# Two query projections of a windowed attention as one pair of seven half products

## The chip, the cores and the metric

The kernel runs on one core of one Trainium2 chip. The metric is device time in microseconds (us), the median of several executions. TensorE does the matmuls, VectorE and ScalarE the element-wise work and the reading of matmul results out of PSUM, and SyncE (SP) issues every transfer, in one queue. GpSimd does next to nothing here.

## The reference

One encoder block on x of 1024 tokens by 1024 features, float32:

```
h = RMSNorm(x)
[g_q, g_k, g_v, g_r, lr_f, lr_b, s_q, s_k, s_v, gate_a, gate_b] = split(h @ w_in)
A = gated linear attention, 4 heads, chunks, both directions     (g_q, g_k, g_v, g_r, lr_f, lr_b)
B = softmax attention, 8 query and 2 key/value heads of 128, blocks of 128 tokens,
    each block sees itself and its two neighbours; RMS-normed and rotated s_q, s_k; a sink logit
x = x + (sigmoid(gate_a) * (A @ w_o_gla) + sigmoid(gate_b) * (B @ w_o_swa)) @ w_out
x = x + (silu(h2 @ w_ff_gate) * (h2 @ w_ff_up)) @ w_ff_out,   h2 = RMSNorm(x)
```

The change concerns `s_q = h @ w`, with w of 1024 x 1024: the queries of the eight softmax heads. The kernel calls its two column halves `sq0` (heads 0 to 3) and `sq1` (heads 4 to 7).

## The kernel before

**Precision.** A float32 operand is split into two float32r parts, high and low: `h` is ScalarE's rounded copy, `l` VectorE's difference (`wunit`, L63 to L70, and `wsplit` for weights; `xsplit` for activations). A product is three matmuls: high x high, high x low, low x high. A weight unit is 128 x 512, 256 KB. The normalised activations are held as `xh`, `xl`: eight feature groups of 128 by two token halves of 512, without the token's inverse norm, which is applied when a result is read out (`rstdt` for token-major, `rstd` for feature-major results).

**Dense work as filler.** A list `dense` holds Python generators, each of which emits one matmul at a time: `proj_t` (token-major projections: v0, v1, skv, sq0, sq1, each once for each token half), `proj_f` (feature-major ones) and `first_halves` (the first product of twelve later pairs, L229). `fill(n)` emits the next n matmuls of that list. TensorE's order is exactly the order in which the code emits (`manual_schedule`). The other engines and the transfers are ordered by a planner, from its own idea of costs and by when operands are ready, except where `keep_in_program_order` or `issue_after` pins an instruction.

The gated attention and then the softmax attention run in numbered slots, as software pipelines. Each slot is cut into stages, and behind each stage a share of dense matmuls is emitted; `GF` and `SF` say how many a slot gets. In slot t of the softmax attention, group n (block n // 2, heads 4(n % 2) to 4(n % 2) + 3) passes: rotation of its queries in slot n + 1 (`a_rope`, VectorE), transposes in n + 2 (`a_turn`, L756, then a split of the result), scores in n + 3 (`a_scores`; VectorE's masked maximum, L774; then ScalarE's exponentials), transposes of the probabilities in n + 4 (`a_probs`, L813, split at L816 and L817), output in n + 5 (`a_out`). `prep(t)` (from L710) loads block t's queries from DRAM. `need(key)` emits twelve dense matmuls at a time until that result has been produced.

**Order of the dense list before:** v0 (both token halves), q1, k1, q2, k2, v1 (both), q3, k3, then for the first token half skv, sq0, sq1, then the same three for the second half, then the first halves. For the first token half `wkeep` splits a weight unit and stores both parts in DRAM (L162); for the second half `wagain` loads them (L170).

**Results through DRAM.** Every projection is read out of PSUM into a staging tile (four buffers), stored, and loaded by its user. x-tiles for loads share three buffers (`xn`).

**Sums of activations.** `x_sums` forms, during gated attention and one step a slot, differences of the normalised activations for the later pairs of seven half products (`xT1`, `x22`, `xT2`, `xT3`, `xT4`) and stores them in DRAM. In the last four slots of the softmax attention, T1 and 22 are loaded and split into the homes of `xh`, `xl` of the second token half (`xpart`, L843, L837).

**Pairs of seven half products.** Some of the later stages already multiply 2 x 2 blocks with seven products in place of eight (`seven`, `pair_T1` and so on).

Of the kernel before, what the change touches and what calls it, by code (L numbers as in the profile page):

```python
# [22 lines left out]
WARM = 10  # L23
GF = ((8, 34), (24, 21), (36, 18), (1 << 30, 11))
SF = ((2, 50), (9, 24), (18, 18), (1 << 30, 12))
PAD = 672
# [4 lines left out]
def body(tc, i, out):  # L31
    nc = tc.nc
    with ExitStack() as root:
# [12 lines left out]
        def mmtile(shape=(P, 512), dt=F32):  # L46
            return psm.tile(list(shape), dt, tag="mm", name=nm("mm"))
# [181 lines left out]
        def first_halves():  # L229
# [4 lines left out]
            def steps():  # L234
                for j in range(0, len(PAIRS), 2):
                    Y = [mmtile(), mmtile()]
                    for u in range(2):
                        for q in range(2):
# [16 lines left out]

        dense = []

# [323 lines left out]
        def g_turn(hd, c):  # L581
# [6 lines left out]
            for j in range(2):  # L588
                nc.sync.dma_start(out=scr["o", 2 * hd + j, c // 4][:, (c % 4) * P:(c % 4 + 1) * P], in_=os_[:, j])

        dense += [proj_t("v0", 0, 0), proj_t("v0", 0, 1), proj_f("q1", 2), proj_f("k1", 3), proj_f("q2", 4), proj_f("k2", 5),
                  proj_t("v1", 1, 0), proj_t("v1", 1, 1), proj_f("q3", 6), proj_f("k3", 7), *(proj_t(nme, n, s) for s in range(2)
                                                          for nme, n in (("skv", 2), ("sq0", 3), ("sq1", 4)))] + [first_halves()]

# [7 lines left out]
        def x_diff(key, k, d, a, b):  # L602
            tc.keep_in_program_order(nc.vector.tensor_tensor(d, a, b, op=ALU.subtract))
            put((key, k), d)

        def x_sums():
            for k in range(KT // 2):
                a = x_norm(k, 0)
# [38 lines left out]
        with tc.manual_schedule(engines={mybir.EngineType.PE}):  # L647
            fill(44)
            for t in range(last + 1):
                work = [[at[t, j]] for j in (0, 5, 4, 3, 2, 1) if (t, j) in at]  # L650
                if t in behind:
                    work = work or [[]]
                    work[-1].append(behind[t])
                slot([lambda v=v: [f(*a) for f, *a in v] for v in work], share(GF, t))
                if t:
                    next(sums, None)
# [147 lines left out]
        def a_probs(g, n, kb):  # L804
# [4 lines left out]
            if kb == a.b0:  # L809
                a.pts = []  # L810
            pt = (mmtile if kb == a.b0 and len(dense) == 1 else chtile)((P, 4, P))
            for h in range(4):
# [7 lines left out]
        def a_out(g, n):  # L820
# [7 lines left out]
            for h in range(4):  # L828
                nc.sync.dma_start(out=scr["b", 4 * g + h, n // 4][:, (n % 4) * P:(n % 4 + 1) * P],
                                  in_=ob[:, h])  # L830

        XT = {q: [] for q in ("T1", "T2", "22", "T3", "T4")}
        def xsplit(pool, th, tl, src):
            h = pool.tile([P, HT], FR, tag=th, name=nm(th))
            l = pool.tile([P, HT], FR, tag=tl, name=nm(tl))
            nc.scalar.activation(h, src, AF.Copy)
            nc.vector.tensor_tensor(l, src, h.bitcast(F32), op=ALU.subtract)  # L837
            return h, l

        homes = {"T1": (xp, "xh{}1", "xl{}1", 0), "22": (xp, "xh{}1", "xl{}1", 4),  # L840
                 "T3": (xp, "xh{}0", "xl{}0", 0), "T4": (xp, "xh{}0", "xl{}0", 4)}

        def xpart(q, k):  # L843
            r = xn.tile([P, HT], F32, tag="xn", name=nm("xn"))
            nc.sync.dma_start(out=r, in_=scr[f"x{q}", k])
            pool, th, tl, d = homes[q]
            XT[q].append(xsplit(pool, th.format(k + d), tl.format(k + d), r))

# [15 lines left out]
        with tc.manual_schedule(engines={mybir.EngineType.PE}):  # L864
            for t, v in enumerate(todo):
# [10 lines left out]
                slot([lambda u=u: [f(*a) for f, *a in u] for u in work], share(SF, t))  # L876
                if t >= 2 * KT + 2:
                    assert len(dense) == 1
                    for q in ("T1", "22"):
                        xpart(q, t - 2 * KT - 2)  # L880
        swas.close()
# [738 lines left out]
```

## Time and profile before

| what | value |
|---|---|
| median of 3 runs | 1607.52 us (1606.2 to 1608.94) |
| the profiled execution | 1607.29 us |
| its span, first to last instruction | 1605.5 us |
| TensorE busy | 1596.9 us (99%), 7532 matmuls |
| VectorE busy | 1209.1 us (75%) |
| ScalarE busy | 903.5 us (56%) |
| moved by transfers | 323.24 MB |

The profile is of one execution. Its own time is what the run took on the device; the span is what lies between its first and last instruction. "Busy" is the union of an engine's instructions; matmuls overlap in it, so a busy TensorE may still start them at different rates. Lines such as L756 are lines of the kernel's file. In a row of a group of instructions stand line, engine, operation, output and inputs, shape and count, then busy us and the mean ns of one, then the idle time of the engine just before them and what ended it. A row of stretches gives the length, the busy time of each engine with its number of instructions, the granted TensorE clock as a share of full speed, the share of the 16 transfer engines and GB/s.

### The profile page before, as it was taken

To read this page: it belongs to the slowest core of one execution; us is meant where nothing else is said; L and a number is where in the kernel's file an instruction comes from. 1 tells how busy PE (TensorE), PEld (TensorE's weight loads), DVE (VectorE), ACT (ScalarE), POOL (GpSimd) and SP (SyncE) were. 2 spreads that over 40 slices of the span, in tenths; PEclk is the share of its full clock that TensorE was granted. 3 is DMA by queue.
4 is the path that set the end of the run, shared out by engine and by line. 5 is a ranking of instruction groups with operands and counts; after the bars stand their busy time and mean duration, and the time that the engine had idled before them with its cause. 6 is when DMAs were issued, how large, how long until landed. Compare 5 with 4: busy or idle time off the path is not lost.

```text
span 1605.5 us, 23093 instructions
## 1 busy us (share of the span) xinstructions
PE 1596.9 (99%) x7532; PEld 1330.1 (83%) x7532; DVE 1209.1 (75%) x2287; ACT 903.5 (56%) x1859; POOL 0.2 (0%) x4
## 2 busy tenths in 40 slices
PE   9999999999999999999999999999999999999999
PEld 6888888888888788888888888888888888888887
DVE  8568888746999678786855877777777878689655
ACT  7456778755998645455633656844444444354442
POOL 0000000000000000000000000000000000000000
PEclk9999999999999999999999999999999999999999
DMA  8856767888544487868733656634344564695433
GB/s 270 301 196 213 248 216 259 285 264 286 173 145 139 152 291 246 273 228 273 243 124 105 220 186 204 202 114 151 112 145 157 191 202 161 207 330 175 151 99 118
DMA packets 197979, 323.24 MB, mean 201 GB/s; under 512 B 23423, under 2 KB 49919, under 8 KB 197858
## 3 DMA queue, kind: packets, MB, share of 16 engines
q1 hardware_dynamic: 197858, 321.77, 60.8%
q8 instruction: 59, 0.97, 0.2%
q14 instruction: 62, 0.51, 0.1%
HBM read 216.29 MB, written 105.39 MB: 200 GB/s over the span
## 4 chain that ended last, share of the span: by engine, by line
PE 95%; DVE 2%; ACT 1%; DMA 1%; issue 0%; SPq 0%; DVEq 0%; ACTq 0%
PE mm L73 22%; PE mm L916 10%; PE mm L915 10%; PE mm L914 10%; PE ch L73 8%; PE mm L1458 7%; PE ch L1458 6%; PE ch L914 5%; PE ch L916 5%; PE ch L915 5%; PE mm L246 4%; PE ch L813 1%; PE ch L585 0%; PE ch L756 0%; PE ch L490 0%
## 5 line engine op out<-in xcount | busy, mean ns | idle before, releaser
L893 ACT ACTIVATE wh<-ws 128x512 fp32r<-128x512 f32 x164 | 103.2, 630 | 157.4 <-PE mm L915 83.8
L73 PE MATMUL mm<-wh,xl 128*128 128x512 f32 x320 | 127.3, 398 | 0.0
L73 PE MATMUL mm<-wh,xh 128*128 128x512 f32 x320 | 126.9, 397 | 0.3 <-ACT lrt L313 0.3
L73 PE MATMUL mm<-wl,xh 128*128 128x512 f32 x320 | 127.1, 397 | 0.0
L894 DVE TENSOR_TENSOR wl<-ws,wh 128x512 fp32r<-128x512 f32 x164 | 112.2, 686 | 15.8 <-ACT wh L893 15.4
L67 ACT ACTIVATE wh<-wr 128x512 fp32r<-128x512 f32 x114 | 71.1, 630 | 55.2 <-issue 16.9
L69 DVE TENSOR_TENSOR wl<-wr,wh 128x512 fp32r<-128x512 f32 x114 | 77.9, 686 | 22.0 <-ACT wh L67 20.5
L893 ACT ACTIVATE wh<-a 128x512 fp32r<-128x512 f32 x66 | 41.6, 632 | 90.3 <-PE mm L1458 42.7
L893 ACT ACTIVATE wh<-wr 128x512 fp32r<-128x512 f32 x76 | 47.9, 631 | 60.9 <-PE mm L915 20.2
L894 DVE TENSOR_TENSOR wl<-a,wh 128x512 fp32r<-128x512 f32 x66 | 45.5, 690 | 40.4 <-ACT wh L893 40.2
L73 PEld LDWEIGHTS mm<-wh,xh 128*128 128x128 f32 x320 | 60.3, 188 | 10.6 <-ACT lrt L313 0.8
L1458 PE MATMUL mm<-hl,wh 128*128 128x512 f32 x176 | 68.6, 390 | 0.0
L1458 PE MATMUL mm<-hh,wl 128*128 128x512 f32 x176 | 68.6, 390 | 0.0
L1458 PE MATMUL mm<-hh,wh 128*128 128x512 f32 x176 | 68.5, 389 | 0.0
L73 PEld LDWEIGHTS mm<-wl,xh 128*128 128x128 f32 x320 | 60.3, 188 | 9.6
L73 PEld LDWEIGHTS mm<-wh,xl 128*128 128x128 f32 x320 | 60.3, 188 | 9.0
L907 DVE TENSOR_TENSOR ws<-wr,wr 128x512 f32<-128x512 f32 x80 | 54.5, 686 | 8.0 <-DMA wr<-in_w_f_dram 4.0
L894 DVE TENSOR_TENSOR wl<-wr,wh 128x512 fp32r<-128x512 f32 x76 | 51.9, 684 | 7.6 <-ACT wh L893 7.0
L1425 DVE TENSOR_TENSOR hl<-hr,hh 128x512 fp32r<-128x512 f32 x77 | 52.8, 686 | 5.1 <-ACT hh L1424 5.1
L1424 ACT ACTIVATE hh<-hr 128x512 fp32r<-128x512 f32 x77 | 47.6, 619 | 7.9 <-DMA hr<-B 4.1
L1458 PE MATMUL ch<-hh,wh 128*128 128x512 f32 x132 | 51.4, 389 | 0.0
L1458 PE MATMUL ch<-hh,wl 128*128 128x512 f32 x132 | 51.4, 389 | 0.0
(449 smaller groups left out, 4910.1 us busy)
## 6 DMA issues: line engine op xcount, KB each, us to landing
wr<-in_w_fi_dram SPq DMA_DIRECT2D x110, 256.0 KB, 4.0
wr<-in_w_f_dram SPq DMA_DIRECT2D x96, 256.0 KB, 3.7
wh<-wh SPq DMA_DIRECT2D x80, 256.0 KB, 3.3
wl<-wl SPq DMA_DIRECT2D x80, 256.0 KB, 3.1
B<-c SPq DMA_DIRECT2D x44, 256.0 KB, 2.1
T<-st SPq DMA_DIRECT2D x44, 256.0 KB, 3.1
a<-in_w_fo_dram SPq DMA_DIRECT2D x44, 256.0 KB, 5.1
hr<-T SPq DMA_DIRECT2D x44, 256.0 KB, 2.7
```

The source lines that it names most:

```text
L67: nc.scalar.activation(h, raw, AF.Copy)
L69: nc.vector.tensor_tensor(l, raw, h.bitcast(F32), op=ALU.subtract)
L73: nc.tensor.matmul(o, a, b, start=start, stop=stop)
L246: nc.tensor.matmul(Y[q], w[:, c], x, start=f0, stop=f1, skip_group_check=True)
L893: nc.scalar.activation(h, src, AF.Copy)
L894: nc.vector.tensor_tensor(l, src, h.bitcast(F32), op=ALU.subtract)
L907: nc.vector.tensor_tensor(t, x, y, op=op)
L914: nc.tensor.matmul(o, h[:, c], x[kk][0], start=start and kk == 0, stop=False, skip_group_check=True)
L915: nc.tensor.matmul(o, h[:, c], x[kk][1], start=False, stop=False, skip_group_check=True)
L916: nc.tensor.matmul(o, l[:, c], x[kk][0], start=False, stop=kk == nk - 1, skip_group_check=True)
L1425: nc.vector.tensor_tensor(l, r, h.bitcast(F32), op=ALU.subtract)
L1458: nc.tensor.matmul(ys[m], a[:, c], b, start=f0, stop=f1, skip_group_check=True)
```

## The change

The projections sq0 and sq1 leave the list as four `proj_t` generators and come back as one generator, `sq_seven`. With the weight and the activations cut into 2 x 2 half blocks, it makes seven products, each of four k-groups by four token tiles: 11 and 21 from the plain activations and weights, T2, T3, T4, T1 and 22 from sums. Three partial results (`sqp`, `squ2`, `squ3`) go through DRAM and come back by `back`. The first query tile of sq0 comes out of the second product, that of sq1 out of the fifth; the second token half's come out of the sixth (sq1) and seventh (sq0). The sums of weights are formed by `w_sums` ahead of the sums of activations, in gated attention, two steps a slot in slots 1 to 15 and one from there on. The activation parts are loaded and split within the products (`part`), the last of them T1 and 22, which stay where the later pairs want them; the loads in the last four slots are gone. The parts of these weights are split anew where they are used and no longer kept in DRAM; skv's two halves now follow one another in the list. The shares `GF` and `SF` are other numbers, and the transposes of probabilities use the other PSUM pool while sq_seven runs and again from the fifth pair of first halves on.

```diff
-GF = ((8, 34), (24, 21), (36, 18), (1 << 30, 11))
-SF = ((2, 50), (9, 24), (18, 18), (1 << 30, 12))
+GF = ((8, 34), (24, 21), (36, 18), (1 << 30, 13))
+SF = ((1, 50), (2, 22), (9, 19), (18, 16), (1 << 30, 8))
@@ first_halves
                     Y = [mmtile(), mmtile()]
+                    if j == len(PAIRS) - 4:
+                        late.append(j)
...
+        def sq_seven():
+            src = (("11", lambda k: i["w_t"][3, k]), ("21", lambda k: i["w_t"][3, k + 4]),
+                   ("T2", lambda k: scr["ws2", k]), ("T3", lambda k: scr["ws3", k]),
+                   ("T4", lambda k: i["w_t"][4, k + 4]), ("T1", lambda k: scr["ws1", k]),
+                   ("22", lambda k: scr["ws4", k]))
+            for _, f in src:
+                plan.extend((lambda k=k, f=f: wunit(f(k))) for k in range(4))
+            S = {q: [] for q in ("T2", "T3", "T4")}
+            S["11"], S["21"] = ([(xh[k + d][0], xl[k + d][0]) for k in range(4)] for d in (0, 4))
+            S["T1"], S["22"] = XT["T1"], XT["22"]
+            held = []
+
+            def part(q, k):
+                d = 0 if q in ("T3", "T1") else 4
+                r = xn.tile([P, HT], F32, tag="xn", name=nm("xn"))
+                nc.sync.dma_start(out=r, in_=scr[f"x{q}", k])
+                S[q].append(xsplit(xp, f"xh{k + d}1", f"xl{k + d}1", r))
+
+            def back(key, t):
+                r = xn.tile([P, HT], F32, tag="xn", name=nm("xn"))
+                nc.sync.dma_start(out=r, in_=scr[key, t])
+                held.append(r)
+
+            extra = {("11", n): [lambda n=n: part("T2" if n < 4 else "T3", n % 4)] for n in range(8)}
+            extra.update({("T3", n): [lambda n=n: part("T4", n)] for n in range(4)})
+            extra.update({("T4", n): [lambda n=n: part("T1", n)] for n in range(4)})
+            for q, v in (("T1", (0, 1, 6, 7)),):
+                for k, n in enumerate(v):
+                    extra.setdefault((q, n), []).append(lambda k=k: part("22", k))
+            for q, key, v in (("21", "sqp", (5, 6, 7)), ("T2", "sqp", (0,)), ("T1", "squ3", (1, 2, 3, 4)),
+                              ("22", "squ2", (1, 2, 3, 4))):
+                for j, n in enumerate(v):
+                    extra.setdefault((q, n), []).append(
+                        lambda t=j + 3 * (q == "T2"), key=key: back(key, t))
+
+            def done(q, t, b):
+                o = stage()
+                if q in ("11", "21"):
+                    nc.scalar.activation(o, b, AF.Copy, scale=rstdt[:, t:t + 1])
+                elif q in ("T1", "22"):
+                    nc.vector.tensor_tensor(o, b, held.pop(0), op=ALU.add)
+                else:
+                    nc.scalar.copy(o, b)
+                put({"11": ("sqp", t), "21": ("sq0", t), "T2": ("squ2", t), "T3": ("squ3", t), "T4": ("sq1", t),
+                     "T1": ("sq1", t + 4), "22": ("sq0", t + 4)}[q], o)
+
+            def steps():
+                b = [mmtile() for _ in range(4)]
+                for q, _ in src:
+                    for n, (ks, t) in enumerate((ks, t) for ks in ((0, 1), (2, 3)) for t in range(4)):
+                        if n % 4 == 0:
+                            us = {k: next_unit() for k in ks}
+                        if q == "T2" and n < 4:
+                            nc.scalar.copy(b[t], held.pop(0))
+                        c = slice(t * P, (t + 1) * P)
+                        for k in ks:
+                            (h, l), x = us[k], S[q][k]
+                            for a, w, f0, f1 in ((x[0], h, k == 0 and q in ("11", "T1"), False), (x[0], l, False, False),
+                                                 (x[1], h, False, k == 3)):
+                                nc.tensor.matmul(b[t], a[:, c], w, start=f0, stop=f1, skip_group_check=True)
+                                yield
+                        if n > 3:
+                            done(q, t, b[t])
+                        for f in extra.get((q, n), ()):
+                            f()
+            return steps()
...
-                      v1, both halves; q3; k3; then per token half skv, sq0, sq1; first_halves()
+                  proj_t("skv", 2, 0), proj_t("skv", 2, 1), sq_seven(), first_halves()]
...
+        def w_sums():
+            def load(n, k):
+                t = xn.tile([P, HT], F32, tag="xn", name=nm("xn"))
+                nc.sync.dma_start(out=t, in_=i["w_t"][n, k])
+                return t
+
+            def form(key, d, x, y, op):
+                tc.keep_in_program_order(nc.vector.tensor_tensor(d, x, y, op=op))
+                put(key, d)
+
+            for k in range(KT // 2):
+                a, c, b = load(3, k), load(4, k + 4), load(4, k)
+                form(("ws1", k), c, b, c, ALU.add)
+                yield
+                form(("ws3", k), b, a, b, ALU.subtract)
+                yield
+                form(("ws2", k), c, c, a, ALU.subtract)
+                yield
+                d = load(3, k + 4)
+                form(("ws4", k), d, d, c, ALU.subtract)
+                yield
+
         def x_sums():
+            yield from w_sums()
...
-                if t:
+                for _ in range(0 if not t else 2 if t < 16 else 1):
                     next(sums, None)
...
-            pt = (mmtile if kb == a.b0 and len(dense) == 1 else chtile)((P, 4, P))
+            pt = (mmtile if kb == a.b0 and len(dense) == 1 and not late else chtile)((P, 4, P))
...
-                if t >= 2 * KT + 2:
-                    assert len(dense) == 1
-                    for q in ("T1", "22"):
-                        xpart(q, t - 2 * KT - 2)
```

More of the change, by code (lines that the diff above doesn't have):

```diff
@@ L254, in first_halves @@
             return steps()
-        dense = []
+        dense, late = [], []
         def fill(n):
@@ L589, in g_turn, with xsplit @@
                 nc.sync.dma_start(out=scr["o", 2 * hd + j, c // 4][:, (c % 4) * P:(c % 4 + 1) * P], in_=os_[:, j])
+        XT = {q: [] for q in ("T1", "T2", "22", "T3", "T4")}
+        def xsplit(pool, th, tl, src):
+            h = pool.tile([P, HT], FR, tag=th, name=nm(th))
+            l = pool.tile([P, HT], FR, tag=tl, name=nm(tl))
+            nc.scalar.activation(h, src, AF.Copy)
+            nc.vector.tensor_tensor(l, src, h.bitcast(F32), op=ALU.subtract)
+            return h, l
+        homes = {"T1": (xp, "xh{}1", "xl{}1", 0), "22": (xp, "xh{}1", "xl{}1", 4),
+                 "T3": (xp, "xh{}0", "xl{}0", 0), "T4": (xp, "xh{}0", "xl{}0", 4)}
@@ new lines, in xpart @@
+        def xpart(q, k):
+            r = xn.tile([P, HT], F32, tag="xn", name=nm("xn"))
+            nc.sync.dma_start(out=r, in_=scr[f"x{q}", k])
+            pool, th, tl, d = homes[q]
+            XT[q].append(xsplit(pool, th.format(k + d), tl.format(k + d), r))
+        def sq_seven():
[12 more added lines that the diff above has]
+                r = xn.tile([P, HT], F32, tag="xn", name=nm("xn"))
+                nc.sync.dma_start(out=r, in_=scr[f"x{q}", k])
+                S[q].append(xsplit(xp, f"xh{k + d}1", f"xl{k + d}1", r))
+            def back(key, t):
+                r = xn.tile([P, HT], F32, tag="xn", name=nm("xn"))
+                nc.sync.dma_start(out=r, in_=scr[key, t])
[41 more added lines that the diff above has]
+            return steps()
@@ L591, in body @@
         dense += [proj_t("v0", 0, 0), proj_t("v0", 0, 1), proj_f("q1", 2), proj_f("k1", 3), proj_f("q2", 4), proj_f("k2", 5),
-                  proj_t("v1", 1, 0), proj_t("v1", 1, 1), proj_f("q3", 6), proj_f("k3", 7), *(proj_t(nme, n, s) for s in range(2)
-                                                          for nme, n in (("skv", 2), ("sq0", 3), ("sq1", 4)))] + [first_halves()]
+                  proj_t("v1", 1, 0), proj_t("v1", 1, 1), proj_f("q3", 6), proj_f("k3", 7),
+                  proj_t("skv", 2, 0), proj_t("skv", 2, 1), sq_seven(), first_halves()]
@@ L830, in a_out @@
                                   in_=ob[:, h])
[L832 to L847, printed above, removed]
         todo = [[] for _ in range(2 * KT + 6)]
```

## The prediction

> **What bounds the kernel now.** I read the page of the profile first: busy shares, the forty slices, the chain that ended last.
>
> ```profile
> PE 1596.9 (99%) x7532; PEld 1330.1 (83%) x7532; DVE 1209.1 (75%) x2287; ACT 903.5 (56%) x1859; POOL 0.2 (0%) x4
> ...
> PE   9999999999999999999999999999999999999999
> ...
> DVE  8568888746999678786855877777777878689655
> ACT  7456778755998645455633656844444444354442
> ...
> PEclk9999999999999999999999999999999999999999
> DMA  8856767888544487868733656634344564695433
> ...
> PE 95%; DVE 2%; ACT 1%; DMA 1%; issue 0%; SPq 0%; DVEq 0%; ACTq 0%
> ```
>
> TensorE is never idle and the chain lies on it, so a matmul removed is time saved, if nothing else becomes late. But in slices 10 to 12 (400 to 520 us, the softmax attention) VectorE stands at 9 and ScalarE at 8 to 9: there three engines are full at once. This case is decided there. Next I took the price of a matmul from the chain in order of time, and engine sums by stretch of the attention stage.
>
> ```profile
> 1452.26 29.92 PE mm L1458 x132
> ...
> 364.00:404.00 40.00, 39.32 (x200) 33.05 (x199) 27.51 (x86) 25.25 (x63) 0.00 (x0) 1.00 0.85 285
> 404.00:529.00 125.00, 125.00 (x685) 107.94 (x684) 118.76 (x335) 116.38 (x284) 0.00 (x0) 1.00 0.48 150
> 529.00:553.00 24.00, 22.92 (x119) 18.18 (x118) 15.30 (x39) 16.84 (x42) 0.00 (x0) 1.00 0.34 110
> sum 189.00, PE 187.24 PEld 159.16 DVE 161.56 ACT 158.47 POOL 0.00; mean PE 62.41 PEld 53.05 DVE 53.85 ACT 52.82 POOL 0.00
> ```
>
> A 128x512 matmul costs 29.92/132 = 0.2267 us of TensorE. The columns of the stretches are length, then PE, PEld, DVE, ACT, POOL busy, granted clock, DMA share, GB/s. From 404 to 529 VectorE works 118.76 of 125 us (95%) and ScalarE 116.38 (93%), and TensorE still loses nothing.
>
> **The change, part by part.**
>
> *Matmuls.* Four projections of 8 x 4 x 3 = 96 become seven half products of 4 x 4 x 3 = 48: 384 become 336. 48 x 0.2267 = 10.9 us less on TensorE, all on the path. With nothing else the profiled execution, 1607.29 us, would become 1596.4. The attention's and the gated attention's matmuls stay.
>
> *Work ahead of the attention.* The weight sums are 16 VectorE operations, 16 loads and 16 stores, handed out in the first eight slots of gated attention; the activation sums move later, two steps a slot up to the fifteenth.
>
> ```profile
> 60.00:80.00 20.00, 20.00 (x96) 16.71 (x96) 10.03 (x20) 7.71 (x15) 0.00 (x0) 1.00 0.94 323
> 80.00:100.00 20.00, 20.00 (x105) 17.06 (x104) 13.05 (x28) 11.32 (x23) 0.00 (x0) 1.00 0.61 202
> 100.00:140.00 40.00, 40.00 (x220) 34.58 (x219) 28.71 (x59) 19.03 (x45) 0.00 (x0) 1.00 0.60 198
> ...
> 300.00:340.00 40.00, 39.38 (x213) 32.85 (x214) 21.35 (x55) 28.47 (x85) 0.00 (x0) 1.00 0.84 279
> ...
> L598 DVE SCALAR_TENSOR_TENSOR xn<-xn,g,rstd x16: 729/747/752, 57.6 to 294.7; 128x512 f32<-128x512 f32 x16
> ...
> 357.82 0.68 DVE L679 TENSOR_TENSOR kA<-cosb,kg 128x512 f32<-128x512 f32 x1
> 358.42 0.68 DVE L680 SCALAR_TENSOR_TENSOR kB<-sinb,kg 128x512 f32<-128x512 f32 x1
> ```
>
> The sixteen normalisations run from 57.6 to 294.7, slots 1 to 27, so a slot is some 9 us and the first eight end near 125 us. Back to back, VectorE starts a 128x512 operation every 358.42 - 357.82 = 0.60 us although one lasts 0.68 (0.605 is taken). 16 x 0.605 = 9.7 us: from 60 to 140 VectorE is busy 51.8 of 80 us, so it is covered. If that cover were gone it would cost up to those 9.7. The 32 transfers of 256 KB are 8.4 MB in some 65 us, 129 GB/s more; on 198 to 202 they fit below the 323 that the first stretch moves, but in that first stretch they queue. SP is one queue in order: a weight load behind a store that waits for its sum would be late. Bounds: 0 and, if in 60 to 80 the transfers run one slot late, some 1.5 us; I take 0.3. Against it stands the end of gated attention, where TensorE idles 0.62 us from 300 to 340 and now has 13 dense matmuls a slot instead of 11: between 0 and -0.6, I take -0.3. They cancel.
>
> The dropped copies are 16 units x 2 stores and 2 reloads, 64 transfers. Added are 32 for the sums, 12 unit loads, 12 parts, 12 reloads and 12 more stores of partial results, 80: 16 x 0.256 = 4 MB more of 323. Inside the seven products each bank is read out 18 matmuls (4.1 us) before it is written again, and one read-out takes under 0.7 us (row below): hidden, and exposed only if ScalarE is 3 us behind.
>
> *When the attention can start.* Its first query tile needs both projections, and the second half of the pair now comes from the fifth of the seven products. I counted the dense matmuls in program order from the loops. Before, the first query transpose stands behind 1110 of 1536. Now that tile is finished behind the 1086th of 1488 (with 12 at a time until it is there), and the first transpose stands behind the 1124th.
>
> ```profile
> 378.54 0.60 PE L756 MATMUL ch<-ident,qr 128*128 128x128 f32 x4
> ...
> L221 ACT ACTIVATE st<-mm,rstdt 128x512 f32<-128x512 f32 x40 | 27.4, 685 | 5.3 <-PE mm L73 5.3
> ...
> L222 SPq DMA_DIRECT2D sq<-st x16: 319/320/382, 308.5 to 436.7; - x16
> ...
> DMA to landing us min/median/max: 2.0/3.0/4.3
> ...
> L717 SPq DMA_DIRECT2D qr<-sq x16: 319/424/1501, 359.7 to 490.2; - x16
> ...
> DMA to landing us min/median/max: 2.6/3.2/4.9
> ...
> 553.24 1.38 PE ch L73 x6
> 554.62 14.53 PE mm L246 x64
> ```
>
> Before, the transpose came at 378.54. The 1086th matmul lies 24 x 0.2267 earlier, at 373.1. Behind it: 0.69 of read-out, a store (median 3.0) and a load (3.2); with the issues on SP and the hand-overs some 8 us, so the query lands at 381.2. TensorE reaches its transposes at 378.54 + 14 x 0.2267 = 381.7, and the rotation on VectorE needs about 1.9 first (two half-width and two full operations), so TensorE waits some 1.4 us at once. At the slowest landings of both rows it would be 3.0 more.
>
> *VectorE in the attention.* Between the first transpose and the last output (553.24) stood 362 dense matmuls and now stand 303. Unhindered, TensorE would be there 59 x 0.2267 = 13.4 us sooner: 381.7 + 174.7 - 13.4 = 543.0. VectorE has the same attention to do, but in the 161.8 us from 381.2 instead of 189. Its dense operations in the old 189 us, weight splits (L69), read-outs (L249) and activation splits (L837), were 23 + 18 + 8:
>
> ```profile
> 364.00:553.00 189.00, 15.67 (x23) 1.00 0.54 174
> ...
> 364.00:553.00 189.00, 12.35 (x18) 1.00 0.54 174
> ...
> 364.00:553.00 189.00, 5.42 (x8) 1.00 0.54 174
> ...
> 470.09 0.69 DVE L760 TENSOR_TENSOR sql<-ch,sqh 128x512 fp32r<-128x512 f32 x1
> ...
> 474.98 0.33 PE L73 MATMUL ch<-kTh,sqh 128*128 128x384 f32 x1
> ```
>
> Now they are the same 41 for the first halves (227 dense matmuls behind the pair by the last output, 224 before), 6 weight splits and 4 activation splits of the last two products, and 8 additions that read their banks out: 59, ten more, 6.1 us. The key rotation of one block (about 1.5) can go ahead of the query's landing. So VectorE needs 161.6 + 6.1 - 1.5 = 166.2 us where TensorE would give 161.8. That is the low bound of the wait, and 3 splits (1.8) can slip past the end: 2.6. The high bound goes by the last transpose, after which the stage is a chain of waits (15.30 of 24 us busy). Up to there VectorE must do 161.6 - 15.3 + 6.1 - 1.5 + 1.2 (one unit more by then) = 152.1; TensorE would be there at 529 + 3.2 - 50 x 0.2267 = 520.9, 139.7 us after 381.2. At the 95% of the stretch from 404 to 529 VectorE takes 160.1: 20.4 us late. At 100% it is 12.4. Off this goes what VectorE may fall behind before TensorE feels it: the split query ended at 470.78 and was used at 474.98, 4.2 us of lead, and the 1.8. So 6.4 at 100%, 14.4 at 95%, with ends 2.6 and 20.4. I take 12, nearer to 14.4, because that row is the same work. ScalarE loses the scaled read-outs of the old projections and four of eight activation splits, and gets six weight splits and three read-outs: by estimate some 155 us (158.5 in the sum row) of 161.8, hardly a bound of its own.
>
> [...]
>
> *The end of the stage.* 61 dense matmuls then stand behind the last output instead of 64, so the next stage's loads have about the cover they had; the eight activation splits no longer fall into the last slots. Nothing is charged.
>
> **Sum.** 1607.29 - 10.9 (matmuls) + 12 (VectorE late in the attention) + 0.3 - 0.3 = 1608.4. The median shown is 0.23 above the profiled execution: 1608.6.
>
> **The rivals.** (A) *The lead pays the backlog: faster.* Besides the 4.2 us, VectorE works far ahead in places:
>
> ```profile
> 423.37 0.69 DVE L699 TENSOR_TENSOR qr<-qr,rq 128x512 f32<-128x512 f32 x1
> ...
> 448.44 0.60 PE L756 MATMUL ch<-ident,qr 128*128 128x128 f32 x4
> ...
> L73 PE MATMUL ch<-ph,vSh 128*128 128x512 f32 x3 | 1.3, 431 | 0.8 <-ACT ph L816 0.8
> ```
>
> A rotation ended at 424.06 and its transposes came at 448.44, 24 us on. If the instruction order lets VectorE put the urgent operations first and keep no gap, the wait is the low bound plus the first 1.4, about 4: 1600.5. Against it: the tail already waits 0.8 us on the probability split (last row) with VectorE idle, so the order is not free of gaps. (B) *Nothing of the lead can be used: slower.* VectorE and ScalarE wait for each other at 95 and 93%; the whole 20.4 shows: 1607.5 - 10.9 + 20.4 = 1617. It decides from 14.1 us of wait (10.9 + 3.2). For it: in 404 to 529 both engines are that full while TensorE gave them 125 us for 12 slots, and now each slot is 0.45 to 1.1 us shorter (two to five dense matmuls less). Against it: those cuts also take dense work off VectorE. (C) *The first query is late as well*, at the slowest landings: VectorE starts 3.0 later, 1611.6. [...]
>
> **How the numbers follow.** Forecast (wait of 7.7 to 14.1 us, within 0.2%): 0.32, since the middle of the bounds lies there. A: 0.33, B: 0.30, C: 0.05. 0.2%, 3.2 us, is about what a measurement of this kernel can tell from no change. So faster 0.33, same 0.32, slower 0.35. The forecast's own range is 1604.3 to 1610.7. For 8 in 10 it reaches to A's 1600.5 and a little below, as a wait of 2.6 gives 1599.2, and to B's 1617: 1599 to 1617. Left out are the full 10.9 us (1596.6) and a wait above 20.
>
> **What would show it.** Right: 48 fewer 128x512 matmuls; the first query transposes near 382 to 384 with some idle before them on the rotation; between them and the last output VectorE above 95% busy, and TensorE idle in many short pieces ended by VectorE or ScalarE, 8 to 14 us together; stretches before 370 and after the stage without new idle time. Wrong: TensorE without idle time there (A), idle over 14 us (B), one idle piece above 3 us ahead of the first transpose (C), or idle time in the first eight slots behind late weight loads, which I priced at 0.3. The sum also falls if VectorE's operations run in another order than program order suggests, since the non-TensorE engines are ordered by the planner.

## The result, and the profile after

The changed kernel takes **1619.42 us** (1616.96 to 1622.15), the kernel before 1607.60 beside it: ratio 1.0074, 95% interval 1.0056 to 1.0092. It is slower by some 12 us, outside the predicted range (1599 to 1617). The profiled execution took 1619.05 us with a span of 1617.2, 11.7 more than before.

The page of the changed kernel, the lines that answer to those shown of before:

```profile
PE 1595.2 (99%) x7484; PEld 1321.7 (82%) x7484; DVE 1236.2 (76%) x2335; ACT 920.1 (57%) x1891; POOL 0.2 (0%) x4
...
PE   9999999998999999999999999999999999999999
...
DVE  8578898758999677776855877677677888689655
...
PE 82%; ACT 6%; DVE 5%; DMA 5%; issue 2%; SPq 1%; ACTq 0%; DVEq 0%
```

The 48 matmuls are gone (7532 to 7484). But the chain that ended last lies on TensorE for only 82% (95% before): it now runs through VectorE, ScalarE and a DMA as well. The slices hide this, since an idle piece of 3 us is less than a tenth of a slice.

Engine sums by stretch show the place. The stretches are cut at the first query transposes, the fifth, the sixteenth and last, and the last output of the attention. First the kernel before, then the changed one (columns as in the prediction):

```profile
378.50:414.50 36.00, 35.32 (x190) 30.11 (x189) 30.16 (x97) 28.08 (x72) 0.00 (x0) 1.00 0.72 238
414.50:529.00 114.50, 114.50 (x630) 98.92 (x629) 108.30 (x304) 107.97 (x262) 0.00 (x0) 1.00 0.48 148
529.00:554.50 25.50, 24.42 (x126) 19.38 (x125) 15.30 (x39) 16.84 (x42) 0.00 (x0) 1.00 0.37 121
```

```profile
389.00:430.20 41.20, 35.72 (x169) 28.47 (x170) 38.03 (x109) 29.91 (x77) 0.00 (x0) 0.92 0.60 189
430.20:542.90 112.70, 110.02 (x599) 92.33 (x598) 105.66 (x303) 100.97 (x246) 0.00 (x0) 1.00 0.42 133
542.90:567.40 24.50, 22.60 (x117) 17.79 (x116) 13.56 (x38) 18.11 (x45) 0.00 (x0) 1.00 0.38 117
```

The stage has 59 fewer dense matmuls, 13.4 us of TensorE, and it isn't shorter: 178.4 us for 176.0. The first four groups became 5.2 us longer with 21 fewer matmuls, VectorE 92% busy (38.03 of 41.20) and the granted clock at 0.92. And the first transposes come 10.5 us later (389.0 for 378.5).

What TensorE waits for: the four longest of the changed kernel's list, and ahead of them the two longest of the kernel before (total, times, longest):

```profile
PE mm L73 <- DVE ones L84: 1.0, 1, 1.0
PE ch L73 <- ACT ph L816: 0.8, 1, 0.8
```

```profile
PE ch L73 <- DVE pl L926: 3.8, 8, 1.4
PE ch L73 <- DVE sql L869: 3.5, 1, 3.5
PE ch L865 <- DVE qr L808: 3.2, 1, 3.2
PE ch L73 <- DVE tl L539: 1.3, 1, 1.3
```

Nothing of the kernel before's list is longer than 1.0. The four lines of the changed kernel are all ended by VectorE: the probability split, the query split, the rotation ahead of the first query transposes, and a split in gated attention.

**An account of the loss.** For each kernel of the table I worked out TensorE's lost time from its trace: for each matmul, the time from its start to the next one's, less what such a pair of shapes usually takes (the 20th percentile in that trace). It counts idle time and half clock alike. *Ahead* is all up to 5 us before the first query transposes; *first* from there to the fifth transposes, *middle* to the sixteenth, *end* to the last output, *behind* the rest. *Dense* is the number of dense matmuls in the stage's three stretches, first, middle and end. In e6 *end* holds a wait of 6.8 us that begins right behind the last output.

| kernel | dense: first / middle / end | stage, us | lost: ahead | first | middle | end | behind |
|---|---|---|---|---|---|---|---|
| before | 98 / 214 / 50 | 175.9 | 17.5 | 2.4 | 5.9 | 3.2 | 4.0 |
| changed | 78 / 184 / 41 | 178.4 | 21.4 | 15.5 | 10.8 | 4.2 | 3.5 |
| e11_half | 91 / 191 / 49 | 176.2 | 17.9 | 3.0 | 11.8 | 3.8 | 3.6 |
| e9_oldnew2 | 78 / 196 / 41 | 178.2 | 16.7 | 7.1 | 15.0 | 4.2 | 4.8 |
| e13_anew | 98 / 214 / 50 | 177.4 | 16.1 | 3.4 | 6.3 | 3.2 | 3.6 |
| e6_newold | 98 / 214 / 30 | 181.9 | 23.2 | 12.3 | 7.7 | 8.9 | 6.4 |
| e10_inside | 91 / 208 / 42 | 185.3 | 21.6 | 12.5 | 15.0 | 1.6 | 9.0 |
| e12_early | 91 / 208 / 42 | 186.8 | 20.5 | 11.5 | 11.2 | 5.7 | 4.3 |
| e14_early2 | 78 / 184 / 41 | 180.8 | 21.0 | 17.7 | 10.4 | 4.2 | 3.7 |
| e15_earlyrel | 78 / 184 / 41 | 172.1 | 21.0 | 8.7 | 10.9 | 1.5 | 3.6 |
| e7_relief2 | 78 / 184 / 41 | 172.9 | 22.5 | 14.9 | 7.4 | 2.0 | 3.7 |
| e8_pool | 78 / 184 / 41 | 182.1 | 19.7 | 15.8 | 16.2 | 2.5 | 4.1 |

From before to changed the losses grow by 3.9 + 13.1 + 4.9 + 1.0 - 0.5 = 22.4 us. TensorE's work shrinks by 10.6. The sum, 11.8, is the 11.7 of the spans. The experiments ask what makes the 22.4.

### The profile page after: what moved, and what is told of

Read it like the earlier page. It is cut to its first block, busy times and chain, and to the rows that moved or that the text cites. A ratio compares the mean times of both kernels' runs of the same rounds, so it can differ in the third digit from the quotient of the medians.

```text
span 1617.2 us, 23137 instructions
## 1 busy us (share of the span) xinstructions
PE 1595.2 (99%) x7484; PEld 1321.7 (82%) x7484; DVE 1236.2 (76%) x2335; ACT 920.1 (57%) x1891; POOL 0.2 (0%) x4
## 4 chain that ended last, share of the span: by engine, by line
PE 82%; ACT 6%; DVE 5%; DMA 5%; issue 2%; SPq 1%; ACTq 0%; DVEq 0%
PE mm L73 13%; PE mm L1004 10%; PE mm L1002 10%; PE mm L1003 10%; PE mm L1546 7%; PE ch L1546 6%; PE ch L73 5%; PE ch L1004 5%; PE ch L1002 5%; PE ch L1003 5%; PE mm L248 3%; PE mm L669 1%; DMA xn<-in_w_t_dram 1%; ACT p L905 1%; ACT p L911 1%
## 5 line engine op out<-in xcount | busy, mean ns | idle before, releaser
L67 ACT ACTIVATE wh<-wr 128x512 fp32r<-128x512 f32 x126 | 78.5, 628 | 63.5 <-issue 16.9
L69 DVE TENSOR_TENSOR wl<-wr,wh 128x512 fp32r<-128x512 f32 x126 | 85.9, 686 | 28.4 <-ACT wh L67 26.3
L981 ACT ACTIVATE wh<-wr 128x512 fp32r<-128x512 f32 x76 | 47.9, 631 | 59.5 <-PE mm L1003 20.2
L73 PE MATMUL mm<-wl,xh 128*128 128x512 f32 x192 | 76.3, 398 | 0.0
L73 PE MATMUL mm<-wh,xh 128*128 128x512 f32 x192 | 75.8, 395 | 0.3 <-ACT lrt L315 0.3
L73 PE MATMUL mm<-wh,xl 128*128 128x512 f32 x192 | 75.9, 395 | 0.0
L982 DVE TENSOR_TENSOR wl<-wr,wh 128x512 fp32r<-128x512 f32 x76 | 52.0, 685 | 7.8 <-ACT wh L981 7.1
L73 PE MATMUL mm<-xl,wh 128*128 128x512 f32 x128 | 50.7, 396 | 0.7 <-DVE xl L332 0.7
L1546 PE MATMUL ch<-hl,wh 128*128 128x512 f32 x132 | 51.3, 389 | 0.0
L73 PE MATMUL mm<-xh,wh 128*128 128x512 f32 x128 | 50.3, 393 | 0.2
```

The source lines that it names most:

```text
L67: nc.scalar.activation(h, raw, AF.Copy)
L69: nc.vector.tensor_tensor(l, raw, h.bitcast(F32), op=ALU.subtract)
L73: nc.tensor.matmul(o, a, b, start=start, stop=stop)
L1546: nc.tensor.matmul(ys[m], a[:, c], b, start=f0, stop=f1, skip_group_check=True)
```

## The experiments

Differences of the changed kernel's variants of under some 3 us are within its own spread (1617 to 1622), so several verdicts rest on the traces. The kernel before, measured beside every run, took 1606.7 to 1607.6.

**The late first tile by itself.** Two runs on what the first idle pieces cost. One (e1) fills them with spare matmuls on data that lie ready (16 ahead of the first query transposes, 16 ahead of the second group's first scores, results unused); one (e2) gives the second slot more dense work:

```
+            if n == 0 and g == 0: spare(16)       # in a_turn; in a_scores the same for g == 1
```


> The changed kernel with 16 spare 128x512 matmuls ahead of the first query transposes and 16 ahead of the second group's first scores, where TensorE stands idle 3.2 and 3.5 us; their result is not used. Theory L (the first query tile is late, and TensorE's clock falls behind the idle pieces): the granted clock stays 1.00 from 380 to 420 us and the slow matmuls behind the two idle pieces, about 4 us, are won: 1615 to 1616. Theory V (VectorE has more to do in the attention than time, and TensorE waits for it whatever its clock): the clock stays 1.00 but the time is unchanged, 1619 to 1620.

```
-SF = ((1, 50), (2, 22), ...   +SF = ((1, 50), (2, 46), ...
```


> The changed kernel with 46 instead of 22 dense matmuls in slot 1 of the attention, which then are missing at its end. 24 x 0.2267 = 5.4 us of useful work are put where TensorE waits 3.2 us for the first rotation. L: first wait and slow clock gone, 1611 to 1613. V: VectorE starts when it did, so TensorE's later waits grow less but stay; only the work moved into the wait counts, 3.3 to 5.4 us: 1614 to 1616, with the wait on the second split query still there.

Measured: 1617.67 (ratio 1.0066, 1.0053 to 1.0078) and 1619.27 (1.0078, 1.0066 to 1.0091). The spare matmuls hold the clock at 1.00 where the changed kernel had 0.92 (first stretch of each):

```profile
387.50:426.80 39.30, 36.07 (x185) 29.27 (x184) 36.67 (x105) 29.32 (x75) 0.00 (x0) 1.00 0.67 214
```

yet the stage lasts 178.1 us for 178.4: this stretch is 1.9 us shorter and the rest nearly as much longer. So the half clock is a symptom here, as far as this run shows: TensorE runs slowly where it would otherwise have waited. With more cover in slot 1 (dense matmuls that TensorE can do while it would otherwise wait) the first wait goes and others come, 2.0 for the query split and 3.0 for the row maximum (L883), and the stage lasts 178.7.

**VectorE by itself.** Leave out 20 low parts on VectorE (e3: 12 activation parts of T4, T1 and 22, 8 weight parts of T1 and 22; the high part stands in), and, in another run (e4), let the planner place the weight sums freely:

```
-    plan.extend((lambda k=k, f=f: wunit(f(k))) for k in range(4))
+    plan.extend((lambda k=k, f=f, q=q: (high if q in ("T1", "22") else wunit)(f(k))) for k in range(4))
...
+    S[q].append((h, h) if q in ("T4", "T1", "22") else xsplit_low(h, f"xl{k + d}1", r))
```


> The changed kernel without 20 of VectorE's low parts in the pair: for the activation parts of T4, T1 and 22 and the weights of T1 and 22 the high part stands in for the low part, so the result is another one; matmuls, loads and ScalarE's work stay. 20 x 0.605 = 12 us less on VectorE between about 370 and 420 us. V: the second wait (3.5 us) and a good part of the 6 us of short waits from 420 to 560 go, 1610 to 1613. L: the first tile is as late as before and the clock falls as before; 1617 to 1619.

```
-    tc.keep_in_program_order(nc.vector.tensor_tensor(d, x, y, op=op))
+    nc.vector.tensor_tensor(d, x, y, op=op)
```


> The changed kernel with the 16 sums of weights no longer pinned in VectorE's order. At 128 us VectorE waited 1.34 us for the load of one and TensorE 1.6 + 0.5 us for the operation behind it. If the pinned order did that: those 2.1 us go, 1617 to 1618. If not: 1619 to 1620.

Measured: 1620.41 (1.0080, 1.0067 to 1.0092) and 1617.61 (1.0068, 1.0054 to 1.0082). Twelve microseconds less of VectorE gave nothing; the waits moved. From this I took VectorE's rate for innocent, too early, as the run e15 below shows: most of what was left out lay ahead of the first transposes, and in the first stretch VectorE was busy only 2.9 us less (35.12 for 38.03). In the second run the wait on L539 is gone from the list, but from 100 to 140 us TensorE lost 2.4 us all the same, for 2.9 in the changed kernel: fixing the sums in VectorE's order isn't by itself the cause.

**The shares by themselves.** The change also altered how many dense matmuls a slot gets. Four kernels separate that from the seven products: the old products with the new shares (e5, and e9 with the transposes in the other pool), the new products with the old shares (e6), and the old products with two thirds of the move (e11, which has e9's edit for the pool as well).

```
-GF = (..., (1 << 30, 11))   SF = ((2, 50), (9, 24), (18, 18), (1 << 30, 12))
+GF = (..., (1 << 30, 13))   SF = ((1, 50), (2, 22), (9, 19), (18, 16), (1 << 30, 8))
```


> The kernel before with only the two lines of shares of the change: 59 fewer dense matmuls lie between the first query transposes and the last output, and as many more behind or ahead of the stage; nothing else differs. Theory S (the attention stage, 176 us before and 178 after, is as long as the chain of its first groups and VectorE make it; its dense matmuls are cover, and TensorE stands idle where they are taken out): stage 170 to 176 us, and the 13.4 us come back as time: 1615 to 1621. Theory T (TensorE sets the stage as long as the first query is in time): stage 162 to 164, time unchanged, 1606 to 1609.

> The changed kernel with the old shares: 50 dense matmuls in slot 1, 24 and 18 in the later ones, so that the dense list runs out before the stage ends. S: the stage stays near 178 us with less idle time in it, up to where the list is empty; some 60 dense matmuls, 13 us, move from outside into it, less what the empty end costs: 1608 to 1612. T: every matmul costs what it did, only the first wait goes: 1614 to 1617.

```
+    if j == len(PAIRS) - 6: late.append(j)     # ... and "and not late", as in the change
```


> The kernel before with the changed kernel's shares alone (its seven half products are not in it), and with the probability transposes taking their PSUM tile from the other pool for the last pairs. By count 315 dense matmuls lie inside the attention stage in place of 362, and 121 behind it in place of 64. Theory S (the stage lasts about 176 to 178 us whatever dense work lies in it, and work taken out is paid in full): 47 x 0.2267 = 10.7 us more, 1616 to 1621. Theory T (TensorE is the bound; work that leaves the stage shortens it): 1606 to 1609.

```
-SF = ((2, 50), (9, 24), (18, 18), ...   +SF = ((2, 50), (9, 22), (18, 16), ...
```


> The kernel before with about two thirds of the same move: by count 331 dense matmuls inside the stage in place of 362, and 96 behind it in place of 64. Theory S: 31 x 0.2267 = 7.0 us more, 1612 to 1616, and between the kernel before and the run with 315. Theory T: 1606 to 1609.

Measured: new shares alone 1620.75 (1.0082, 1.0069 to 1.0096) and, with the other pool, 1622.56 (1.0097, 1.0083 to 1.0111); in these two a part of the output has other values, every instruction being issued as counted. Two thirds of the move: 1613.59 (1.0040, 1.0026 to 1.0053). The middle stretch of e11 and of e9:

```profile
413.80:529.10 115.30, 111.61 (x606) 93.78 (x605) 105.84 (x305) 106.99 (x259) 0.00 (x0) 1.00 0.44 137
```

```profile
411.70:531.30 119.60, 114.79 (x611) 95.73 (x610) 106.17 (x301) 108.36 (x260) 0.00 (x0) 0.99 0.44 137
```

With 362, 331 and 315 dense matmuls inside, the stage lasts 175.9, 176.2 and 178.2 us. It doesn't shrink with TensorE's work. What is taken out is paid in full elsewhere: 31 x 0.2267 = 7.0 (measured 6.9), 47 x 0.2267 = 10.7 (measured 13.7 to 15.9, the stage being 2.3 longer as well). That is theory S, and T, by which moved work costs nothing, falls. The new products with the old shares were to take 1608 to 1612 and took 1622.49 (1.0099, 1.0085 to 1.0113): there the list of dense work ran out before the stage's end (by count none is left behind it, 61 in the changed kernel), the stage took 181.9 us where theory S had 178, and TensorE waited for the next stage's weights:

```profile
PE ch L1002 <- ACT wh L981: 6.8, 1, 6.8
```

**More dense work inside the changed kernel's stage**, without (e10) and with an early first tile (e12):

```
-SF = (..., (9, 19), (18, 16), (1 << 30, 8))   +SF = (..., (9, 22), (18, 18), (1 << 30, 8))
```


> The changed kernel with shares that put 341 dense matmuls inside the stage in place of 303, and 22 behind it in place of 61. Theory S: the stage stays at 178 to 181 us and the 38 matmuls are hidden in it, 8.6 us less, of which 4 to 6 are lost again at the end, where the list is nearly empty: 1612 to 1616. Theory T: the stage becomes 8.6 us longer and the time stays at 1618 to 1620.

```
-    need((f"sq{g}", t))
+    key = (f"sq{g}" if t > 3 else "sq0", t); need(key)      # and loads scr[key]
```


> As the run with 341 inside, and the first four blocks take the tiles of the other query product (heads 0 to 3 in place of 4 to 7), which are stored long before, so that no first query is waited for; their queries are not the reference's. Theory that the late first tile costs its wait and VectorE's lead: 3 to 5 us less than the run with 341 inside, 1608 to 1612. If the first tile costs nothing beyond what slots lose anyway: as that run, 1612 to 1616.

Measured: 1623.59 (1.0101, 1.0088 to 1.0115) and 1614.69 (1.0051, 1.0038 to 1.0065). Theory S missed the first: the stage grew to 185.3 us, nearly as T had it, and behind it 5.5 us more were lost (9.0 for 3.5), which T hadn't.

```profile
430.60:552.90 122.30, 117.02 (x622) 98.24 (x623) 111.07 (x312) 104.94 (x253) 0.00 (x0) 0.99 0.41 131
```

With the products, dense work inside the stage isn't cover alone: it brings splits and read-outs. VectorE was busy 153.8 of 176.0 us before, 157.3 of 178.4 in the changed kernel and 161.5 of 185.4 here, 87 to 88% each time, which suggests that the stage's length goes with VectorE's work. But not with it alone: with the old products and fewer dense matmuls VectorE's work fell to 149.5 (e11) and 150.1 us (e9), 84 to 85% of the stage, and the stage got no shorter; ScalarE kept its 152 there. In all eighteen kernels the busier of the two stands at 85 to 89% of the stage. That is a pattern; no run shows what holds them there. The early tile gains 8.9 in the medians where 3 to 5 were expected, and 6.7 in the spans of the two traces, 4.7 of it behind the stage: with the tile there sooner, 24 matmuls that had been handed out while it was missing lie there, and the loss falls from 9.0 to 4.3.

**VectorE's rate in the middle**: 24 low parts of the first halves' weights left out (e7), and the same 24 on GpSimd (e8).

```
-    plan.extend((lambda r=PAIRS[j + q][2], u=u: wunit(i["w_f"][r, u])) for q in range(2))
+    ... high(i["w_f"][r, u]) ...     # the other run: wunit(..., eng=nc.gpsimd)
```


> The changed kernel with the high part standing in for the low part of the first halves' weights, so that their result is another one: 24 VectorE operations of 0.605 us fewer, about 20 of them between 420 and 565 us; matmuls and ScalarE's work stay. If VectorE's rate sets slots 6 to 17 (112.7 us, 105.7 of them busy): up to 6 us are won, the middle falls to 106 to 108 us, 1613 to 1615. If the waits there are a chain's: 1618 to 1620.

> The changed kernel with the same 24 subtractions made by GpSimd, which is idle, in place of VectorE; the result is the same. If VectorE's rate sets the slots and GpSimd is not in its way: as with VectorE relieved of them, 1613 to 1616. If GpSimd is slower than 3 us for one, TensorE waits for the weights: above 1620.

Measured: 1614.18 (1.0048, 1.0036 to 1.0061) and 1624.05 (1.0107, 1.0093 to 1.0121).

```profile
430.70:540.10 109.40, 108.90 (x600) 92.79 (x599) 95.10 (x281) 101.40 (x246) 0.00 (x0) 1.00 0.43 135
```

```profile
L69 POOL TENSOR_TENSOR wl<-wr,wh 128x512 fp32r<-128x512 f32 x24 | 31.3, 1313 | 540.0 <-DVE mx L883 398.4 <-ACT wh L67 132.3 <-DMA b<-st 6.4
```

In the middle VectorE's rate does count: 10.6 us less work there (95.10 for 105.66) made the stretch 3.3 us shorter and took 3.4 of the loss. On GpSimd one of these subtractions takes 1313 ns where VectorE takes 686, and the middle became 5.5 us longer. VectorE wasn't relieved by it: with 18 operations fewer it was busy 106.48 us there, and 95.10 in e7. Its large operations kept their lengths, but small ones grew, above all this one (the changed kernel, then e8, in the middle stretch):

```profile
L898 DVE SCALAR_TENSOR_TENSOR mx<-mx,rs 128x4 f32<-128x4 f32 x11 | 1.7, 153 | 0.0
```

```profile
428.90:547.10 118.20, 111.66 (x600) 91.83 (x599) 106.48 (x285) 101.77 (x247) 20.55 (x16) 1.00 0.41 127
...
L898 DVE SCALAR_TENSOR_TENSOR mx<-mx,rs 128x4 f32<-128x4 f32 x11 | 6.8, 616 | 0.0
```

All eleven overlap in time with a subtraction on GpSimd. So this run says nothing against VectorE's rate as the bound of the middle.

**What remained**, the first four groups and the time ahead. Four runs: the kernel before with only the splits made anew (e13); the changed kernel with the early tile (e14); the early tile and the relief of e3 together (e15); and no weight sums (e16).

```
-    plan.extend((lambda k=k: (wkeep, wagain)[s](n, k)) for k in range(KT))
+    plan.extend((lambda k=k: wunit(i["w_t"][n, k]) if n > 2 else (wkeep, wagain)[s](n, k)) for k in range(KT))
```


> The kernel before with one part of the change alone: the weight parts of the pair's 16 second-half units are not read back from DRAM but split anew, 16 operations each on VectorE and ScalarE, of which 10 to 12 fall into the first four groups of the attention. Dense matmuls and first tile as before. Theory V (VectorE's added work in the first groups makes the idle time there): 10 x 0.605 us at about 90% is 6.7 us more of VectorE work in 36 us where it was busy 30: 3 to 6 us slower, 1610 to 1613. Theory C (the late tile or the missing cover makes it): 1606 to 1609.

The next two have the edit of e12, the second that of e3 as well.

> The changed kernel with its own shares; the first four blocks take the tiles of the other query product, so the first tile is not waited for (the queries of heads 4 to 7 of these blocks are not the reference's). If the late tile costs its wait and what VectorE loses by it: 3.3 to 7 us less, 1612 to 1616. If it costs nothing beyond: 1618 to 1620.

> As the run before, and 20 low parts on VectorE are left out (12 activation parts of T4, T1 and 22, 8 weight parts of T1 and 22; the high part stands in for the low one). Theory V: the idle time of the first four groups falls to that of the kernel before, 5 to 8 us less than the run with the early tile alone, 1606 to 1610. If neither VectorE nor the tile makes the idle time: within 2 us of it.

```
-    ("T2", lambda k: scr["ws2", k]), ("T3", lambda k: scr["ws3", k]), ...
+    ("T2", lambda k: i["w_t"][4, k]), ("T3", lambda k: i["w_t"][4, k]), ...
```


> The changed kernel without the 16 weight sums and their loads and stores; the products read the weights themselves in their place (other values, the same matmuls). If the sums make the idle time at 120 to 140 us and after: 2 to 3.5 us less, 1616 to 1617.5. If not: 1618.5 to 1620.5.

The kernel before doesn't feel 16 splits more: 1607.30, ratio 1.0007 (0.9999 to 1.0016). It makes them in time that VectorE has free ahead of the first tile; its stage is 1.5 us longer, and it loses 1.4 less ahead. The last 10 us ahead of the first query transposes, of the kernel before and of this one:

```profile
368.50:378.50 10.00, 10.00 (x46) 8.20 (x46) 5.18 (x12) 1.59 (x5) 0.00 (x0) 1.00 1.02 361
```

```profile
367.20:377.20 10.00, 10.00 (x47) 8.19 (x46) 9.92 (x26) 5.89 (x15) 0.00 (x0) 1.00 0.64 190
```

The early tile alone: 1620.34 (1.0091, 1.0077 to 1.0105), no gain, like the relief alone. **Both together: 1610.58 (1.0026, 1.0016 to 1.0035), 8.8 us less than the changed kernel.** The first four groups, with the early tile and with both:

```profile
382.50:426.60 44.10, 36.68 (x169) 29.65 (x170) 39.56 (x115) 29.63 (x75) 0.00 (x0) 0.89 0.65 208
```

```profile
379.90:417.50 37.60, 33.86 (x169) 27.34 (x168) 33.43 (x103) 31.63 (x82) 0.00 (x0) 0.95 0.80 264
```

The same 169 matmuls take 37.6 us instead of 44.1, and the loss falls from 17.7 to 8.7 (15.5 in the changed kernel, 15.1 with the relief alone), near the 7.1 of the old products with as few dense matmuls (e9); 2.7 more go at the stage's end. The time lies just above theory V's 1606 to 1610. This fits two causes side by side in the first groups, each of which hides the other: a late tile, before which VectorE can do little of the attention, and VectorE's added work behind it. Either one taken away leaves the other as the bound, so single removals show nothing. One thing isn't separated: the planner also put VectorE's operations in another order. With the early tile alone the queries had landed by 372.85, but their rotation, behind other operations, ended only at 382.43, and TensorE still waited 2.6 us for it; with both it ended at 375.34 and nothing waited. How much of the 8.8 is less work and how much this order stays open.

Without the weight sums: 1616.86 (1.0065, 1.0052 to 1.0077), 2.6 less. From 120 to 140 us, the changed kernel and this one:

```profile
120.00:140.00 20.00, 18.31 (x100) 15.54 (x100) 16.82 (x36) 9.42 (x22) 0.00 (x0) 1.00 0.90 297
```

```profile
120.00:140.00 20.00, 20.00 (x114) 17.39 (x113) 15.30 (x33) 10.21 (x24) 0.00 (x0) 1.00 0.50 172
```

That is the wait of 1.3 us in the list above, and its cause is one row of the changed kernel's order in time:

```profile
129.37 0.69 DVE L699 TENSOR_TENSOR xn<-xn,xn 128x512 f32<-128x512 f32 x1 [1.34 <-DMA xn<-in_w_t_dram]
129.98 0.48 DVE L539 SCALAR_TENSOR_TENSOR tl<-pf,dec,th 128x256 fp32r<-128x256 f32 x1
```

A weight sum, fixed in VectorE's order, waits for its load, and the split (L539) that TensorE needs stands behind it. This is one way in which the sums cost time and not the only one, as e4 shows. That they are the cause all the traces together show: from 100 to 140 us TensorE loses 2.2 to 6.7 us in each of the twelve kernels that form the weight sums, and 0.8 in each of the six that don't.

## Why the prediction was wrong

*Matmuls, -10.9*: right. 48 are gone, and the work measured in the three stages shrinks by 10.6.

*Work ahead of the attention, 0.3 - 0.3*: wrong by 3.9. It was priced as VectorE time, 9.7 us under cover, and as transfers; the prediction named a late weight load but priced it at 0.3, with 1.5 as the bound. The sums cost 2.1 in the trace (2.9 lost from 100 to 140 us, 0.8 before), 2.6 in the medians (e16). The other 1.4 lie from 280 to 360 us (6.5 lost, 5.1 before), where 13 matmuls a slot were to save 0.3. It is neither these shares (4.2 with them and the old products, e9) nor the sums (6.2 without them, e16); what it is wasn't tried.

*The first query*: the count was right and the step behind the landing wrong. With 3.9 us lost ahead, the landing predicted at 381.2 becomes 385.1; it came at 384.9. TensorE's arrival, 381.7, becomes 385.6; it came at 385.8. But from the landing to the transposes I had 1.9 us for the rotation, and it took 4.0:

```profile
378.73 0.76 DVE L805 TENSOR_TENSOR rq<-qr,qB 128x256 f32<-128x256 f32 x2
...
384.95 1.06 ACT L827 ACTIVATE sq<-qr 128x1024 f32<-128x1024 f32 x1 [1.95 <-DMA qr<-sq]
386.04 1.49 DVE L835 TENSOR_REDUCE ss<-sq 128x10 f32<-128x1280 f32 x1 [2.30 <-ACT sq L827]
387.44 0.68 DVE L807 TENSOR_TENSOR qr<-qr,qA 128x512 f32<-128x512 f32 x1
388.23 0.68 DVE L808 TENSOR_TENSOR qr<-qr,rq 128x512 f32<-128x512 f32 x1
388.96 0.66 PE L865 MATMUL ch<-ident,qr 128*128 128x128 f32 x4 [3.19 <-DVE qr L808]
```

VectorE put the sum of squares, 1.49 us and not needed until the softmax, between the parts of the rotation, and stood idle 2.30 before it. The rotation writes over the queries in place (`a.qn = a.qr`), so it couldn't go on before ScalarE had squared them, and one operation squares all eight heads. So heads 0 to 3, whose rotation VectorE had begun at 378.73, waited for the tile of heads 4 to 7. Squares of four heads at a time might lift this; it wasn't tried. The wait was 3.2, not 1.4.

*VectorE in the attention, +12*: this is the step that failed. With the first wait in it, as the prediction had it, the term measured 13.1 + 4.9 + 1.0 = 19.0, near the high bound of 20.4. I took 12 by crediting 4.2 us of lead and 1.8 of slip and leaning towards 14.4. There was little lead to credit (rival C inside rival B): from the end of a rotation to its transposes the first four groups had 0.1, 8.9, 9.5 and 11.2 us, where the kernel before had 7.5, 15.6, 9.1 and 15.6. Nor was VectorE's work too much for the time: from the landing to the last output it was busy 160.20 us, where I had 166.2, against 161.8 that TensorE was to give. It took 182.25 us over it, 88%, and the bounds had assumed 95 to 100%. So the size came out near a bound by luck; the reason behind it, a lack of VectorE time, doesn't hold over the whole stage. Nor was the loss where I looked for it, building up to the last transpose: 13.1 of it fell into the first four groups. The middle, for which I had argued with 95%, kept its 94% (105.66 of 112.70).

The premise behind it failed too. "TensorE would be there 59 x 0.2267 = 13.4 us sooner" treats the stage's dense matmuls as its bound. In the kernel before they were cover: without the products, moving 31 out left the stage at 176.2 us for 175.9 (e11). The rows quoted then, VectorE 95 and ScalarE 93% with TensorE full, said that three engines were balanced, so that removing TensorE's work alone need not gain anything. I read them as a question of how late VectorE would be. With the measured terms the sum comes out: 1607.29 - 10.6 + 3.9 + 19.0 - 0.5 = 1619.1, for 1619.05 profiled.

*ScalarE hardly a bound*: in the changed kernel's stage it was busy 148.99 of 178.4 us (155 of 161.8 estimated), less than VectorE, which agrees. *The end of the stage, nothing*: right, 3.5 lost behind it for 4.0.

Of the rivals B came nearest: 1617 for 1619.42. Of its 20.4 nearly all showed, though not for its reason; what it lacked was the 3.9 ahead. A fell: with the first tile missing VectorE had little to do ahead, though it works ahead where nothing is missing (e13). C's lateness came, by the rotation and not by slow landings.

*The clock.* The forecast has no term for it: in every row of stretches quoted of before the granted clock is 1.00. In the changed kernel it fell: behind the 3.19 us piece the granted clock is 0.70 for the stretch from 388 to 392 us and TensorE starts its matmuls 0.43 us apart for 0.23. By e1, with the clock at 1.00 there, it cost the stage nothing (178.1 us for 178.4).

What stays open: why neither VectorE nor ScalarE passes 89% over the stage, what of e15's gain is less work and what the order of VectorE's operations, and the 1.4 us from 280 to 360. No version that ran beats the kernel before; e13, nearest to it, equals it.

## What to carry to other kernels

Where a stretch shows three engines nearly full at once (here TensorE 100, VectorE 95 and ScalarE 93%), removing TensorE's work from it may be worth nothing, until a run with the same work moved out shows that the stretch gets shorter; that run (e11: 31 matmuls out, 176.2 us for 175.9) needs a few changed shares and would have decided this case. A product scheme whose second half has its first output only in the fifth product can delay the first consumer, and engines that were ahead can lose their lead there (here 0.1 us of it ahead of the first transposes for 7.5). When one removal changes nothing, try the two suspects together before acquitting either (here 1620.34 and 1620.41 us one at a time, 1610.58 together).

## What the runs showed of the hardware

In these kernels the granted clock fell behind idle pieces of 3.19 us (the changed kernel) and less, and the length of a piece doesn't decide by itself. In the old products with the new shares (e9) a single piece of 1.85 us was enough; where the 16 splits are made anew (e13), one of 1.7 us wasn't. The 4 us behind each:

```profile
376.00:380.00 4.00, 2.45 (x9) 2.06 (x10) 3.93 (x10) 2.26 (x4) 0.00 (x0) 0.76 0.93 320
```

```profile
392.00:396.00 4.00, 4.00 (x25) 3.45 (x24) 3.52 (x16) 2.42 (x6) 0.00 (x0) 1.00 0.29 85
```

But without the 24 low parts (e7) a piece of 3.51 us, from 402.45 to 405.95, left the clock at full speed:

```profile
404.00:408.00 4.00, 2.04 (x12) 1.87 (x13) 2.84 (x9) 1.86 (x3) 0.00 (x0) 1.00 1.01 372
408.00:412.00 4.00, 3.12 (x17) 1.90 (x16) 4.00 (x12) 2.27 (x9) 0.00 (x0) 1.00 0.83 275
```

The records of the granted clock show a pattern that all three fit. Inside the kernels every slow stretch lasts 3.41 us, or twice or three times that, at half clock; the changed kernel has two, from 389.64 and from 406.71 us. If each of the fifteen traces that have such stretches is laid out in intervals of 3.413 us that meet their starts, every interval in which TensorE was busy less than 44% of the time is followed by a slow one, and none in which it was busy more than 68%; between them both occur. In the changed kernel the two slow stretches follow intervals in which TensorE was busy 20 and 36%. The 1.85 us lie in one interval, which was 46% busy, and the 3.51 us are shared by two, 1.80 and 1.70. What sets the length of these intervals, and the two shares, no run shows.
